# Gate-branch products woven into block 2's attention, and x and the first weights loaded in K pairs over two DMA queues

## The chip, the core and the metric

The kernel runs on one core of a Trainium2 chip. TensorE (PE) multiplies; VectorE (DVE), ScalarE (ACT) and GpSimd (POOL) work on tiles; SyncE (SP) issues nearly all DMAs. The metric is the device time of one execution in microseconds, as the median of several runs. PSUM holds the products, SBUF everything else.

## The reference

Two models run in a row on 256 rows of width 1024. The first has two layers: an RMS norm, a mixer of three attention branches with sigmoid gates, and a convolutional feed-forward. Its output goes through a final norm into the second, which has two layers over latents (256 rows) and a context (256 rows). The part that the change touches most is the second model's layer:

```
z = modulate(rmsnorm(x), shift, scale) @ w_in      # q, k, v, u, g for latents; context too, except in the last layer
attn = softmax(rope(rms(q)) rope(rms(k))^T) v      # 8 heads of 64; latents see 512 keys, the context 256
gm   = gelu(u) * (w_s @ layernorm(gelu(g)) + b_s)  # the gated branch ("gmlp"), 4 groups of 128 columns
x    = x + gate * (concat(attn, gm) @ w_out)
x    = x + gate2 * (square(relu(modulate(rmsnorm(x)) @ w_ff1)) @ w_ff2)
```

[...]

## The kernel before

`program` builds the instructions, and a scheduler orders them on each engine by priority (program order, unless `tc.high_priority` shifts it) and by when its own model of time holds them ready. That order is then fixed: each engine works through its queue in order. A tile pool gives `bufs` slots for each tag, and an instruction waits for a free slot.

**Weights.** `load_w` (line 134) starts one DMA of 1 MB from SP into `raw` (three slots), casts each half on ACT into `hi` (L147, 128x1024) and subtracts on DVE into `lo` (L149). With `by_piece`, used for the very first weights alone, each half has its own DMA, and the last two pairs of x tiles are loaded between them (L115). `mm3` (L157 to L159) issues the three passes of one K tile.

**Start.** `norm` (L451) splits each of the eight x tiles, scaled by the norm's gain, into the parts `e` (L184 on ACT, L185 on DVE), squares and adds them (L441, L443), and makes the row of inverse norms (L193 to L205). Then it loads the second weights and builds the normalised parts `h` (L466, L181, L182). Weight chunks below `EARLY` = 2 multiply `e` and scale the product by the row afterwards (L510); the others need `h`. In layer 0 the first chunk goes tile by tile, so all eight K tiles of its first half come before its second half; in layer 1 `zpair` takes both halves together, six K tiles and then two.

**Block 2, one layer.** After q, k and v come the g products (`g_half`, two halves of two groups each, GELU on ACT at L970). Then, in program order: the layer norm of g (L1049 to L1055), the u products (`u_tasks`: four tiles of eight K tiles, three passes, for each stream, 192 products in layer 0, which has two streams, and 96 in layer 1, which has one; GELU on ACT at L1066), and the attention. `attn` has a `front` (scores into `s`, row maximum on DVE at L1099, exponential on ACT at L363, scaling on ACT at L374) and a `back` (`pair_out`, L379): for each group of two key tiles, four transposes into `pt` (L388), a cast on ACT and a subtraction on DVE into two `kf` tiles (L181, L182), and six products with v into `o`. `pt` has one slot in PSUM, `s` two, `acc` four, and `kf` (the tag of `tmp()`) ten slots in SBUF. `pipelined` emits front i, then back i-1. A latent step has two groups, a context step one: 24 groups in layer 0 (8 latent and 8 context steps), 16 in layer 1 (8 latent steps).

`weave(attn(), fill, ratio)` takes `ratio` items of filler after each step. The filler is `mix_tasks` (four items, small products at L1077 and three DVE steps up to L1083 that build the gated branch) and then `out_half(1)` (eight tiles of 12 products, whose results update x at L1130). `out_half(1)` needs all four mix items.

```
def weave(main, side, ratio):
    due = 0.0
    for _ in main:
        due += ratio
        while due >= 1.0:
            next(side, None)
            due -= 1.0
    run(side)
```

Of the kernel before, what the change touches and what calls it, by code (L numbers as in the profile page):

```python
# [11 lines left out]
F32 = mybir.dt.float32  # L12
# [7 lines left out]
P = 128  # L20
# [9 lines left out]
EARLY = 2  # L30
# [9 lines left out]
WV2 = (0.78, 1.62)  # L40
# [5 lines left out]
XF = 4  # L46

WL = (1.0, 0.75)

PIPE = 1  # L50

# [20 lines left out]
def program(tc, A, out, stop=None):  # L72
# [10 lines left out]
    with top:  # L83
# [27 lines left out]
        par1 = const("par1")  # L111

        def load_x(k0, k1):
            for k in range(k0, k1, 2):
                nc.sync.dma_start(xx[:, k : k + 2, 0:T], A["xT"][:, k : k + 2, :])  # L115

        load_x(0, XF)
        ident = mk(cp, [P, P], tag="ident")
        make_identity(nc, ident)
        ones = mk(cp, [P, P], tag="ones")  # L120
        V.memset(ones, 1.0)
# [8 lines left out]


        last_lo, pin = [None], [None]

        def load_w(ap, *cuts, by_piece=False):

            raw = mk(wp, [P, 2048], tag="raw", bufs=3)
            if not by_piece:
                nc.sync.dma_start(raw[:, : cuts[-1]], ap)
            pieces, a = [], 0
            for b in cuts:  # L140
                if by_piece:
                    nc.sync.dma_start(raw[:, a:b], ap[:, a:b])
                    if a == 0:
                        load_x(XF, KD)
# [234 lines left out]
        def pair_out(po, ps, v, n):  # L379
# [3 lines left out]
            for g in range(0, n, 2):  # L383
# [50 lines left out]
        def block1():  # L434
            with ExitStack() as st:
# [15 lines left out]
                def norm(g, ap):  # L451
# [18 lines left out]
                for l in range(L):  # L470
# [13 lines left out]
                    def zpair(w, x):  # L484
                        ps = [acc()[:, :T] for _ in range(2)]
                        mm_pair(ps, w, x)
                        return ps

                    mod_rate(R1[l][0])
                    w0 = load_w(A["w_in"][l, 0], 1024, 2048, by_piece=l == 0)  # L490
# [4 lines left out]
                    hb = small([P, 24], tag="hb", bufs=2)  # L495
                    V.tensor_scalar_mul(hb, bgate, 0.5)
                    e, h, row, w1 = norm(n1g, A["w_in"][l, 1])


# [4 lines left out]
                    for c in range(3):  # L504
                        w = (w0, w1)[c] if c < 2 else wi(c)
                        first = zpair(w, e) if c == 0 and l else None
                        for mi in range(2):
                            j = 2 * c + mi
                            if c < EARLY:
                                V.tensor_mul(cz[:, j, :], first[mi] if first else ztile(w[mi], e), row)  # L510
# [862 lines left out]
```

## Time and profile before

| | us |
|---|---|
| median of 3 runs | 1806.24 |
| lowest and highest | 1802.46, 1807.23 |
| the profiled execution, its own time | 1804.39 |
| its span, first to last instruction | 1802.6 |
| PE busy in the span | 1750.1 (97%) |
| DVE busy | 1449.8 (80%) |
| ACT busy | 1014.0 (56%) |

The span is 1.8 us shorter than the execution's own time, and that execution is 1.85 us below the median. A PE that is shown busy is not PE at its peak: the end of a product is modelled, and a product after an idle stretch is shown longer than its step in a dense stream. So work on PE is counted below as products times the step from one start to the next in a dense stream.

### The profile page before, as it was taken

The page shows a single profiled execution, that of the slowest core. Times are in us where ns is not written, and L with a number is a line of the kernel's source. Part 1 is how long each engine was busy: PE and PEld are TensorE (multiplying, and loading weights), DVE is VectorE, ACT ScalarE, POOL GpSimd, SP SyncE. Part 2 cuts the span into 40 slices and gives each one's busy share as a digit, 9 for nine tenths or more (in the row PEclk, how much of TensorE's full clock was granted, in tenths as well). Part 3 has the DMA queues.
Part 4 walks back from the last instruction along what each step waited for, and adds up shares of the span by engine and source line. Part 5 has one row for each costly group of instructions (what it writes and reads, how often), then busy time and mean ns, then how long its engine had stood idle before and what let it go on. Part 6 is the DMA issues. An engine that isn't in the chain of part 4 may idle for free.

```text
span 1802.6 us, 33988 instructions
## 1 busy us (share of the span) xinstructions
PE 1750.1 (97%) x13352; PEld 1669.1 (93%) x13352; DVE 1449.8 (80%) x3142; ACT 1014.0 (56%) x1994; POOL 83.0 (5%) x85
## 2 busy tenths in 40 slices
PE   7999999999999999999999899999999999799999
PEld 6999999999999999999999677989898989689999
DVE  7996989889898788988778676988676768777665
ACT  5866656665585665766554575515151536665553
POOL 0100210000010021000012000000000001000000
PEclk9999999999999999999999999999999999999999
DMA  7364664557545456554533221554545443225552
GB/s 283 123 212 165 211 233 171 186 164 257 197 159 199 163 183 246 185 190 158 195 138 119 71 71 36 168 201 154 185 149 191 141 151 117 71 72 209 187 187 94
DMA packets 68096, 297.10 MB, mean 165 GB/s; under 512 B 7648, under 2 KB 11104, under 8 KB 42336
## 3 DMA queue, kind: packets, MB, share of 16 engines
q1 hardware_dynamic: 67936, 294.93, 47.4%
q8 instruction: 105, 1.72, 0.4%
q14 instruction: 55, 0.45, 0.1%
HBM read 293.85 MB, written 1.05 MB: 164 GB/s over the span
## 4 chain that ended last, share of the span: by engine, by line
PE 82%; DVE 9%; ACT 5%; issue 2%; POOL 1%; DMA 1%; SPq 0%; POOLq 0%; ACTq 0%; DVEq 0%
PE acc L157 24%; PE acc L158 23%; PE acc L159 23%; DVE lo L149 2%; PE s L157 2%; PE s L158 2%; PE s L159 2%; PE pt L388 1%; ACT hi L147 1%; DVE u L182 1%; PE o L158 1%; ACT p L363 1%; DVE mjunk L257 1%; ACT p L374 1%; PE o L157 1%
## 5 line engine op out<-in xcount | busy, mean ns | idle before, releaser
L157 PE MATMUL acc<-u,hi 128*128 128x256 f32 (+2 forms) x3604 | 1052.3, 293 | 17.5 <-ACT hi L147 10.3
L159 PE MATMUL acc<-u,lo 128*128 128x256 f32 (+2 forms) x3604 | 1048.7, 292 | 2.6 <-DVE lo L149 2.4
L158 PE MATMUL acc<-u,hi 128*128 128x256 f32 (+2 forms) x3604 | 1051.0, 292 | 0.0
L147 ACT CAST hi<-raw 128x1024 fp32r<-128x1024 f32 (+2 forms) x470 | 473.6, 1010 | 452.9 <-PE acc L158 383.8
L157 PEld LDWEIGHTS acc<-u,hi 128*128 128x128 f32 x3604 | 682.6, 190 | 33.5 <-ACT hi L147 11.4
L159 PEld LDWEIGHTS acc<-u,lo 128*128 128x128 f32 x3604 | 682.4, 190 | 16.7 <-DVE lo L149 4.2
L158 PEld LDWEIGHTS acc<-u,hi 128*128 128x128 f32 x3604 | 683.6, 190 | 13.6 <-DVE u L182 0.6
L149 DVE TENSOR_TENSOR lo<-raw,hi 128x1024 fp32r<-128x1024 f32 (+2 forms) x470 | 552.0, 1182 | 104.5 <-ACT hi L147 100.7
L257 DVE CUSTOM_DVE_ANT_0 mjunk<-mraw,csil,c_par 128x512 bf16<-128x512 f32 x160 | 120.7, 754 | 10.5 <-DMA mraw<-in_w_mod 9.8
L257 DVE CUSTOM_DVE_ANT_0 mjunk<-mraw,csil,mpart 128x512 bf16<-128x512 f32 x160 | 120.8, 755 | 7.9 <-DMA mraw<-in_w_mod 6.5
L1130 DVE SCALAR_TENSOR_TENSOR xx<-acc,mods,xx 128x256 f32<-128x256 f32 x144 | 64.7, 479 | 55.4 <-PE acc L159 55.2
L868 ACT ACTIVATE nt<-nt,shb 128x256 f32<-128x256 f32 x96 | 48.7, 510 | 61.0 <-DVE nt L867 60.9
L181 ACT CAST u<-nt 128x256 fp32r<-128x256 f32 x146 | 57.3, 405 | 41.0 <-DVE nt L1212 33.3
L195 POOL TENSOR_TENSOR rs_y<-rs_v,mhalf 128x2 f32<-128x2 f32 (+2 forms) x26 | 30.9, 1188 | 1019.3 <-DVE rs_v L193 1019.3
L182 DVE TENSOR_TENSOR u<-nt,u 128x256 fp32r<-128x256 f32 x146 | 59.4, 421 | 17.0 <-ACT u L181 15.6
L159 PE MATMUL s<-u,lo 128*128 128x256 f32 x224 | 62.9, 281 | 0.5 <-DVE lo L149 0.5
L157 PE MATMUL s<-u,hi 128*128 128x256 f32 x224 | 62.7, 280 | 0.0
L158 PE MATMUL s<-u,hi 128*128 128x256 f32 x224 | 62.7, 280 | 0.0
L1212 DVE TENSOR_TENSOR nt<-nt 128x256 f32<-128x256 f32 x96 | 40.5, 423 | 19.1 <-ACT nt L868 13.1
L157 PE MATMUL acc<-hi,u 128*128 128x256 f32 (+1 forms) x168 | 48.6, 289 | 0.0
L182 DVE TENSOR_TENSOR kf<-pt,kf 128x512 fp32r<-128x512 f32 x40 | 27.5, 688 | 26.2 <-ACT kf L181 26.0
L159 PE MATMUL acc<-hi,u 128*128 128x256 f32 (+1 forms) x168 | 48.2, 287 | 0.0
(243 smaller groups left out, 2048.7 us busy)
## 6 DMA issues: line engine op xcount, KB each, us to landing
raw<-in_w_ff SPq DMA_DIRECT2D x64, 1024.0 KB, 4.9
raw<-in_w_in SPq DMA_DIRECT2D x61, 1024.0 KB, 4.9
mraw<-in_w_mod SPq DMA_DIRECT2D x192, 256.0 KB, 3.4
raw<-in_w_up SPq DMA_DIRECT2D x44, 1024.0 KB, 4.9
raw<-in_w_down SPq DMA_DIRECT2D x32, 704.0 KB, 4.2
raw<-in_w_out SPq DMA_DIRECT2D x16, 1024.0 KB, 4.9
raw<-in_w_br SPq DMA_DIRECT2D x12, 1024.0 KB, 4.9
nbias<-in_na_bias SPq DMA_DIRECT2D x8, 384.0 KB, 3.0
```

Source lines behind the costliest of these rows:

```text
L147: S.copy(hi[:, : b - a], raw[:, a:b])
L149: last_lo[0] = V.tensor_sub(lo[:, : b - a], raw[:, a:b], hi[:, : b - a].bitcast(F32))
L157: PE.matmul(ps, a[0], b[0], start=start, stop=False)
L158: PE.matmul(ps, a[0], b[1], start=False, stop=False)
L159: return PE.matmul(ps, a[1], b[0], start=False, stop=stop)
L181: S.copy(hi, src)
L182: return V.tensor_sub(lo, src, hi.bitcast(F32))
L195: G.tensor_tensor(y, v, mhalf[:, :n] if len(shape)==2 else mhalf[:, :n].rearrange('p (a b) -> p a b', b=shape[2]), op=ALU.pow)
L257: V.tensor_tensor_reduce(out=junk, in0=w, in1=csil[:, i, half * 512 : half * 512 + 512], op0=ALU.mult, op1=ALU.add, scale=1.0, scalar=part ...
L868: S.activation(dst, dst, func, bias=b)
L1130: V.scalar_tensor_tensor(xx[:, m, cut(s)], ps[:, s * T - cols.start : s * T - cols.start + T], md[i][:, m, s : s + 1], xx[:, m, cut(s)], o ...
L1212: V.tensor_mul(r, r, r)
```

## The change

1. **Start.** `load_first` replaces `by_piece`: for K tiles 0-1, 2-3, 4-5 and 6-7 it loads both halves' columns of the first weights (the first piece from ACT's queue, the others from SP) and the two x tiles. `par1` comes in three DMAs, the eight columns that the first norm needs ahead. `split_first` casts and subtracts those pieces inside `norm`'s loop, and the first products take both halves two K tiles at a time. Four constants (`rope`, `gmask`, `fing`, `par2`) are loaded behind the norm. Eight products of a constant tile run on PE before any data is there.
2. **EARLY** is 3 in block 1's layer 0: chunk 2 multiplies `e` too, and its scaling by the row goes to DVE.
3. **Layer norm of g**: statistics directly behind each g tile, normalisation in two halves, the second behind the first u tile.
4. **u products as filler.** `mix_tasks` now makes the u tiles (`gate_tile`) and each mix one u tile later. Filler items: 16 in layer 0 (one is taken before the attention, then 1.0 a step), 12 in layer 1 (two before, then 1.55 a step). GELU becomes `twice_gelu`: a square and a tanh on ACT, three steps on DVE, with the factor one half in the mix.
5. **`pair_out`**: the six products with v get a priority 40 places later.
6. The attention's output takes the place of `q` (`ya = q`).

```diff
-EARLY = 2
+EARLY = (3, 2)
-WV2 = (0.78, 1.62)
+WV2 = (1.0, 1.55)
+NWARM = 8
+PRE = (1, 2)
+PVO = 40
...
+        idle = mk(pst, [P, 512], tag="pt")
+        for _ in range(NWARM):
+            PE.matmul(idle[:, 0:P], ones, ones, start=True, stop=True)
...
+        def load_first(ap):
+            raw = mk(wp, [P, 2048], tag="raw", bufs=3)
+            pieces = [(mk(wp, [P, 1024], F32R, tag="hi"), mk(wp, [P, 1024], F32R, tag="lo")) for _ in range(2)]
+            view = lambda t: t.rearrange("p (m c) -> p m c", m=2)
+            for k in range(0, KD, 2):
+                cs = slice(k * P, (k + 2) * P)
+                (nc.scalar if k == 0 else nc.sync).dma_start(view(raw)[:, :, cs], view(ap)[:, :, cs])
+                if k == 0:
+                    nc.sync.dma_start(par1[:, 0, 0:8], A["par1"][:, 0, 0:8])
+                load_x(k)
+            nc.sync.dma_start(par1[:, 0, 8:], A["par1"][:, 0, 8:])
+            nc.sync.dma_start(par1[:, 1, :], A["par1"][:, 1, :])
+            return raw, pieces
+        def split_first(raw, pieces, k):
+            for m, (hi, lo) in enumerate(pieces):
+                cs = slice(k * P, (k + 2) * P)
+                src = raw[:, m * 1024 + k * P : m * 1024 + (k + 2) * P]
+                S.copy(hi[:, cs], src)
+                last_lo[0] = V.tensor_sub(lo[:, cs], src, hi[:, cs].bitcast(F32))
...
-        def mm_pair(pss2, pieces, x, order=range(KD), late=2):
-            for part in (order[: KD - late], order[KD - late :]):
+        def mm_pair(pss2, pieces, x, order=range(KD), cuts=(0, 6, 8)):
+            for part in [order[a:b] for a, b in zip(cuts, cuts[1:])]:
...
-                for k in range(2):
-                    c = slice(k * T, k * T + T)
-                    mm3(po, v(g + k), (hi[:, c], lo[:, c]), g + k == 0, g + k == n - 1)
+                with tc.high_priority(offset=-PVO):
+                    for k in range(2):
+                        c = slice(k * T, k * T + T)
+                        mm3(po, v(g + k), (hi[:, c], lo[:, c]), g + k == 0, g + k == n - 1)
...
                     for k in range(KD):
+                        if first and k % 2 == 0:
+                            split_first(*first, k)
                         split(xx[:, k, 0:T], *e(k), g[:, k : k + 1])
...
-                        first = zpair(w, e) if c == 0 and l else None
+                        first = zpair(w, e, (0, 6, 8) if l else (0, 2, 4, 6, 8)) if c == 0 else None
...
+                            elif c < EARLY[l]:
+                                kz = mk(kp, [P, T], tag="nt", bufs=NT)
+                                V.tensor_mul(kz, ztile(w[mi], e), row)
+                                rope(kz, [kpe[:, 0, :], kpe[:, 1, :]], C, Sg, kp, NT)
...
+                    for _ in range(2):
+                        next(second)
+                        next(prep, None)
+                    normalise(0)
+                    weave(second, prep, 1.0)
...
+                    def twice_gelu(dst, x, n):
+                        th = tmp()[:, :n]
+                        S.activation(th, x, AF.Square)
+                        V.tensor_scalar(th, th, 0.044715 * GC, GC, op0=ALU.mult, op1=ALU.add)
+                        V.tensor_mul(th, th, x)
+                        S.activation(th, th, AF.Tanh)
+                        V.scalar_tensor_tensor(dst, th, 1.0, x, op0=ALU.add, op1=ALU.mult)
...
+                        def gate_tile(g):
+                            nonlocal w
+                            if g == 2:
+                                w = load_w(A["w_in2"][l, 4], 1024, 2048)
+                            us[g], ps = tmp(), acc()
+                            for s in streams:
+                                mm_x(ps[:, cut(s)], w[g % 2], (hl, hc)[s], T)
+                                if s != streams[-1]:
+                                    yield
+                            twice_gelu(us[g][:, full], ps[:, full], N)
+                            yield
...
+                        for g in range(4):
+                            yield from gate_tile(g)
+                            if g == 0:
+                                normalise(1)
+                            if g:
+                                mix(g - 1)
+                        mix(3)
...
-                    fill = chain(mix_tasks(), out_half(1, lambda k, c: gm[0](k, c), gate))
-                    run(u_tasks())
+                    fill = chain(mix_tasks(), out_half(1, gm, gate))
                     mod_rate(R2[1])
-                    ya = u8p()
+                    ya = q
+                    for _ in range(PRE[l]):
+                        next(fill)
                     weave(attn(), fill, WV2[l])
```

## Rows read from the trace of the kernel before

**Rows 1.** The page, part 1: busy time, share of the span, instructions of each engine

```profile
PE 1750.1 (97%) x13352; PEld 1669.1 (93%) x13352; DVE 1449.8 (80%) x3142; ACT 1014.0 (56%) x1994; POOL 83.0 (5%) x85
```

**Rows 2.** Windows: length; busy PE, PEld, DVE, ACT, POOL (count); clock, DMA, GB/s

```profile
30.00:60.00 30.00, 29.58 (x243) 28.69 (x242) 28.43 (x67) 17.16 (x36) 5.58 (x6) 1.00 0.59 214
978.00:1000.00 22.00, 22.00 (x187) 22.00 (x186) 18.50 (x59) 5.16 (x7) 3.33 (x1) 1.00 0.44 148
1000.00:1048.00 48.00, 38.76 (x208) 29.45 (x207) 28.84 (x62) 32.01 (x72) 0.00 (x0) 0.97 0.09 32
1048.00:1094.00 46.00, 46.00 (x255) 37.51 (x253) 35.17 (x82) 33.88 (x77) 1.90 (x2) 1.00 0.19 64
1526.40:1541.00 14.60, 13.17 (x106) 12.50 (x105) 11.28 (x44) 6.37 (x11) 3.56 (x3) 1.00 0.36 112
1541.00:1566.00 25.00, 16.71 (x84) 12.17 (x83) 18.00 (x38) 14.71 (x29) 0.29 (x1) 0.93 0.28 104
1566.00:1598.00 32.00, 31.76 (x237) 29.31 (x236) 25.02 (x53) 25.41 (x53) 0.00 (x0) 1.00 0.19 67
1598.00:1607.30 9.30, 6.19 (x38) 4.90 (x37) 2.55 (x5) 2.15 (x5) 0.00 (x0) 0.85 0.00 0
```

**Rows 3.** Two of these windows, scores `s` alone (PE, PEld, DVE, ACT)

```profile
1000.00:1048.00 48.00, 12.36 (x42) 7.49 (x42) 8.95 (x13) 11.35 (x32) 0.97 0.09 32
1541.00:1566.00 25.00, 6.30 (x21) 3.43 (x20) 4.71 (x7) 5.77 (x14) 0.93 0.28 104
```

**Rows 4.** The same two windows, transposes `pt` alone

```profile
1000.00:1048.00 48.00, 7.49 (x44) 5.45 (x44) 7.55 (x11) 6.39 (x11) 0.97 0.09 32
1541.00:1566.00 25.00, 3.42 (x19) 2.58 (x20) 2.75 (x4) 2.31 (x4) 0.93 0.28 104
```

**Rows 5.** The same two windows, products with v, `o`, alone

```profile
1000.00:1048.00 48.00, 12.07 (x60) 8.79 (x60) 2.08 (x5) 2.14 (x6) 0.97 0.09 32
1541.00:1566.00 25.00, 5.53 (x24) 3.98 (x24) 0.00 (x0) 0.10 (x1) 0.93 0.28 104
```

**Rows 6.** The same two windows, `acc` alone (filler and mixes)

```profile
1000.00:1048.00 48.00, 13.34 (x62) 9.14 (x61) 2.98 (x4) 0.59 (x1) 0.97 0.09 32
1541.00:1566.00 25.00, 2.88 (x20) 2.43 (x19) 1.34 (x3) 0.39 (x1) 0.93 0.28 104
```

**Rows 7.** Timeline of PE, layer 0's attention: start, length, instruction, idle before and releaser

```profile
1005.20 0.39 PE L158 MATMUL s<-kk,u 128*128 128x512 f32 x1
1005.43 0.39 PE L159 MATMUL s<-kk,u 128*128 128x512 f32 x1
...
1011.45 0.60 PE L388 MATMUL pt<-ident,kf 128*128 128x128 f32 x4
1012.72 0.38 PE L157 MATMUL o<-kf,vv 128*128 128x256 f32 x1 [0.68 <-ACT kf L181]
...
1014.14 0.60 PE L388 MATMUL pt<-ident,kf 128*128 128x128 f32 x4
```

**Rows 8.** Groups by line and shape, layer 0: busy, mean ns, idle before

```profile
L1066 ACT ACTIVATE u<-acc 128x512 f32<-128x512 f32 x4 | 2.4, 592 | 0.0
...
L1083 DVE TENSOR_TENSOR kf<-kf,u 128x512 f32<-128x512 f32 x4 | 2.7, 685 | 0.1
```

**Rows 9.** Timeline of the start, ACT and PE

```profile
4.36 0.51 ACT L184 ACTIVATE u<-xx,c_par 128x256 fp32r<-128x256 f32 x1 [2.12 <-DMA xx<-in_xT]
...
8.33 1.04 ACT L147 CAST hi<-raw 128x1024 fp32r<-128x1024 f32 x1 [0.89 <-DMA raw<-in_w_in]
...
9.43 0.58 PE L157 MATMUL acc<-u,hi 128*128 128x256 f32 x1 [9.43 <-ACT hi L147]
...
13.42 0.41 PE L159 MATMUL acc<-u,lo 128*128 128x256 f32 x1
...
18.50 0.37 ACT L205 COPY row<-o 128x256 f32<-128x256 f32 x1 [4.43 <-PE o L204]
18.77 2.00 ACT L147 CAST hi<-raw 128x1024 fp32r<-128x1024 f32 x2
```

More of the change, by code (lines that the diff above doesn't have):

```diff
@@ L109, in const, with load_x @@
             return t
[L111 to L117, printed above, removed]
+        par1 = mk(cp, list(A["par1"].shape), tag="c_par1", bufs=1)
+        def load_x(k):
+            nc.sync.dma_start(xx[:, k : k + 2, 0:T], A["xT"][:, k : k + 2, :])
+        ones = mk(cp, [P, P], tag="ones")
+        V.memset(ones, 1.0)
         ident = mk(cp, [P, P], tag="ident")
         make_identity(nc, ident)
-        ones = mk(cp, [P, P], tag="ones")
-        V.memset(ones, 1.0)
         mhalf = mk(cp, [P, 16], tag="mhalf")
@@ L449, in half4, with norm @@
                     return Parts([u8([P, 2, 4, T], F32R)])
-                def norm(g, ap):
+                def norm(g, ap, first=None):
                     e, h = pair8(), pair8()
@@ L482, in ztile, with zpair @@
                         return ps
-                    def zpair(w, x):
+                    def zpair(w, x, cuts=(0, 6, 8)):
                         ps = [acc()[:, :T] for _ in range(2)]
-                        mm_pair(ps, w, x)
+                        mm_pair(ps, w, x, cuts=cuts)
                         return ps
                     mod_rate(R1[l][0])
-                    w0 = load_w(A["w_in"][l, 0], 1024, 2048, by_piece=l == 0)
+                    if l == 0:
+                        first = load_first(A["w_in"][l, 0])
+                        w0 = first[1]
+                    else:
+                        w0, first = load_w(A["w_in"][l, 0], 1024, 2048), None
+                    hb = small([P, 24], tag="hb", bufs=2)
+                    V.tensor_scalar_mul(hb, bgate, 0.5)
+                    e, h, row, w1 = norm(n1g, A["w_in"][l, 1], first)
                     if l == 0:
@@ L970, in g_half, with normalise @@
                             S.activation(vg[0][:, b, c * T : (c + 1) * T], ps, AF.Gelu_apprx_tanh)
+                            for g in range(2):
+                                bn = small([P, 6], tag="bn", bufs=2)
+                                V.bn_stats(bn, vg[0][:, b, c * T + g * P : c * T + (g + 1) * P])
+                                V.bn_aggr(mv[:, b, g, :], bn)
                             yield
+                        rv = rsqrt(mv[:, 0:NB, :, 1], [P, NB, 2], 1.0, EPS)
+                        norms.append((mv, rv))
+                    norms = []
+                    def normalise(c):
+                        mv, rv = norms[c]
+                        for b in range(NB):
+                            for g in range(2):
+                                t = vg[0][:, b, c * T + g * P : c * T + (g + 1) * P]
+                                V.tensor_scalar(t, t, mv[:, b, g, 0:1], rv[:, b, g : g + 1], op0=ALU.subtract, op1=ALU.mult)
                     if l == 0:
@@ L1039, in block2 @@
                     wu = load_w(A["w_in2"][l, 3], 1024, 2048)
-                    weave(g_half(1, wg2), prep, 1.0)
-                    vg = vg[0]
+                    second = g_half(1, wg2)
+                    for _ in range(2):
[3 more added lines that the diff above has]
+                    weave(second, prep, 1.0)
                     if l == 0:
@@ L1070, in block2 @@
-                    gm = []
-                    def mix_tasks():
-                        gm[:] = [u8p()]
-                        for g in range(4):
+                    gm = u8p()
+                    def twice_gelu(dst, x, n):
[5 more added lines that the diff above has]
+                        V.scalar_tensor_tensor(dst, th, 1.0, x, op0=ALU.add, op1=ALU.mult)
@@ new lines, in mix_tasks, with mix @@
+                    def mix_tasks():
+                        us, w = {}, wu
+                        def gate_tile(g):
[9 more added lines that the diff above has]
+                            yield
+                        def mix(g):
```

50 lines of the change are left out of this document (10 added, 40 removed).

## The prediction

> **What bounds the kernel now.** I read the page's busy table first: PE is busy 97% of the span, DVE 80% [rows 1]. So a gain can only come from stretches in which PE stands, and a change that lays work on DVE has to be weighed there. The windows by stage come next, to find those stretches. While the u products run, 187 products take 22.00 us, 0.118 us each, and PE never stands [rows 2]. In layer 0's attention PE is busy 38.76 of 48 us from 1000 to 1048, then 46.00 of 46; in layer 1's 16.71 of 25 us from 1541 to 1566, then 31.76 of 32, then 6.19 of 9.3 [rows 2]. The same loop runs in all of them. What differs is the filler: few big products in the poor windows, many in the good ones [rows 2, 6].
>
> A standing PE is shown too busy, so I count work as products times step. Steps: 0.118 us for 256 columns, 0.23 for 512 (two scores in a row start 0.23 apart [rows 7]), about 0.09 for a transpose (the four at 1011.45 are shown as 0.60, most of it the tail of the last; 0.09 is my estimate, and 0.15 would be its upper end), 0.11 for a 128-column mix, taken as no longer than the 256-column step. Layer 0, 1000 to 1048: 42 scores 9.7, 44 transposes 4.0, 60 products with v 7.1, 32 mixes 3.5, 30 filler products at up to 0.23, 6.9; together 31.2 of 48 us, **16.8 lost** [rows 3 to 6]. Layer 1, 1541 to 1566: 21 scores 4.8, 19 transposes 1.7, 24 products 2.8, 16 mixes and 4 products 2.2; 11.5 of 25, **13.5 lost** [rows 3 to 6]. Around it layer 1 loses 1.4 (1526.4 to 1541), 0.2 and 3.1 more, **18.2** in 80.9 us [rows 2].
>
> Why: with no filler the attention is a ring. One group goes from its transposes at 1011.45 to the next group's at 1014.14, 2.69 us, of which PE works 4 x 0.09 + 6 x 0.118 = 1.07. The products wait 0.68 us for the cast on ACT, and `pt` has one slot, so the next transposes wait too [rows 7]. **1.6 us of each group is exposed.**
>
> At the start PE makes its first product at 9.43 us, behind the cast of the first half megabyte, which ACT begins at 8.33 when the data is there; x was there at 4.36 [rows 9]. At 13.42 a product of 256 columns is still shown at 0.41 us, where one of 512 columns takes 0.39 later [rows 7, 9]: PE is at 1.2 GHz there, the lower of its two levels.
>
> **The change, part by part.**
>
> *Layer 0, u products as filler.* 192 products, 22.6 us, move from ahead of the attention into it; their total stays. They depend on nothing in the attention, so they can lie in the 1.6 us of every group, which the lower priority of the v products asks for. Added on ACT: a square and a tanh where one GELU took 0.592 us, four tiles, +2.4 us; on DVE three steps of 0.685, four tiles, +8.2 us [rows 8]. Counted over 978 to 1094 (116 us), PE's work is 116 - 16.8 = 99.2; DVE's 18.50 + 28.84 + 35.17 + 8.2 = 90.7; ACT's 5.16 + 32.01 + 33.88 + 2.4 = 73.5 [rows 2]. If the stage takes 103 us, DVE is at 88%. That lies between two stages that keep PE full: this loop at 1048 to 1094 with DVE at 76%, and block 1 at 30 to 60 us with DVE at 95% and PE at 29.58 of 30 [rows 2]. So I leave 3.8 us of the 16.8 lost: **-13 us**. Ends: all of it, -16.8; and DVE bound at 76%, 90.7/0.76 = 119 us, +3.
>
> *Layer 1.* 96 products, 11.3 us, move likewise, two of four tiles ahead of the attention. PE's work is 80.9 - 18.2 = 62.7; DVE's 11.28 + 18.00 + 25.02 + 2.55 = 56.9, plus 4 x 3 half-wide steps at half of 0.685, 4.1: 61 us [rows 2, 8]. Now DVE is level with PE. At block 1's 95% the stage would take 64, at the 78% of 1566 to 1598 78 us. I take 72, between them: **-9 us**, ends -17 and -3. ACT has 49.1 us there, 1.0 to 1.8 more with the second table function, and is not the bound [rows 2, 8]. The drain behind the last filler (6.19 busy of 9.3) stays: the last items are given out by step 7 of 8.
>
> *Statistics of g earlier, normalisation in halves:* the same steps on DVE; they leave the front of the attention for the g products. Nothing where DVE has room there, and I credit nothing. `ya = q`: no instruction. The second half of the normalisation now stands in DVE's queue behind the first u tile's three steps, and mixes 2 and 3 wait for it; u tiles 2 and 3 cover that (5.7 us in layer 0).
>
> *The start.* The first K pair is 512 KB with x, so ACT can begin about when it does now, 4.4 to 5 us. From there ACT paces: eight splits and eight squares at no more than 0.51, at most 8.2 us, and 2.0 us of casts (two at 1.00 each, as at 18.77 [rows 9]), up to twice that in quarter tiles: it ends at 15 to 17 us. The first 48 products end 1.4 us later, instead of shortly before 19.8 (the next weights' cast starts at 18.77 and takes 1.0 [rows 9]). Three things decide what is left: whether those casts pass the row copy, which stands 4.43 us at ACT's head [rows 9] (if not, they come up to 1 us later than now, since the row does); that chunk 2 no longer waits for `h`; and that DVE, which gets some 1.7 us more, works at 95% right behind [rows 2]. **-2.5 us**, ends +1 and -5 (first product at 4.4 instead of 9.43). The constants behind the norm pass the second weights in SP's queue; their first user, the rope of chunk 2, is over 15 us away. The DMA issue on ACT stands where ACT waits 2.12 us for x anyway. The eight constant products run before data is there and hold nobody; if they raise the clock, little is won, since ACT needs some 2.5 us for each K pair, and PE's 12 products take 2.8 at twice 0.118.
>
> A rule speaks against the second queue. The row shows the first cast waiting for its data until 8.33 [rows 9]. The Trainium skill, DMA: Bandwidth & Descriptors, section "Issuing engines are not separate DMA queues", has DMAs of all engines share the same 16 engines, so that only issue time is saved. By it the start would come from the order of the pieces alone; if that gave nothing, the sum would be 2.5 us smaller, 22.
>
> **Sum.** -13 - 9 - 2.5 = -24.5. The profiled execution took 1804.4 in all (span 1802.6 and 1.8 around it), so 1779.9; it lay 1.85 below the median of 1806.24, so about **1782** as a median.
>
> **Rivals.**
>
> *DVE takes PE's place.* For: 61 us of DVE against 62.7 of PE in layer 1, 90.7 against 99.2 in layer 0. Against: 95% with PE full at 30 to 60 [rows 2]. Layer 1 gains 3, layer 0 gains 5, the start 2.5: 1796.
>
> *Nearly all is won:* 16.8 + 17 + 5 = 38.8, plus clock, since the windows at 0.93 to 0.97 would stay at 1.00 [rows 2]: about 1766. Against: the drains stay, and each step's chain runs over three engines.
>
> *The start doesn't do what it says,* since w1's casts stay behind the row: 1784 to 1785, inside my range.
>
> *Slower: the queues of ACT and DVE and the ten `kf` slots choke the ring.* GELU's chain now crosses ACT and DVE four times, 2 x 0.592 + 3 x 0.685 = 3.2 us with no handover counted [rows 8], and each link stands ahead of some group's cast. Slots: four score tiles of two steps, four parts of two groups, two u tiles, one for the tanh, one for the mix are 12 of 10. If a group's cast waits behind that chain or for a slot, its 1.6 us is exposed again, filler or not. All 40 groups would cost 64 us; today's loss, 16.8 + 18.2 = 35, is worth 22 groups. Above 22 exposed groups the attention is slower than now; with all 40, +29 - 2.5: 1833. With 30, +13 - 2.5: 1817. Against it: 1048 to 1094 holds the same groups beside filler and loses nothing [rows 2]. The order in a queue does bind: at 18.50 ACT stood 4.43 us at the row while casts that it could have done stood behind [rows 9]. The Trainium skill says that too, in TensorE: Matmul & The Clock Gate, "Architectural detail", where ScalarE's and VectorE's queues are strictly first in, first out; by it each late link would cost what stands behind it, as priced here.
>
> **How the numbers follow.** About 0.3%, 5.4 us, is what a measurement of this kernel can tell from no change. Chances: forecast (1773 to 1790, the start's failure included) 0.55; DVE in PE's place (1790 to 1800) 0.17; nearly all won (below 1773) 0.10; within 5.4 us of now 0.07; slower by the choked ring 0.11. So faster 0.82, same 0.07, slower 0.11. The range 1763 to 1799 leaves out the last two and the edges of the others.
>
> **What would show it.** In the profile after, right: no stretch of the attention in which PE's work is under nine tenths of the time, scores and transposes with `acc` products between, as now at 1048 to 1094; the stretch that is now 978 to 1094 in layer 0 near 103 us instead of 116, layer 1's 1526.4 to 1607.3 near 72 instead of 80.9; the first product at 5 to 6 us, the second chunk's at 16 to 20. Wrong: DVE above 95% in the attention and PE waiting for DVE lines; `o` products still waiting for `kf` casts at L181 in most groups; score products waiting for `kf` slots; a late row in the start. The forecast falls if the scheduler's model puts the u products in one block ahead of the attention, as it could if it believes the ring free of gaps: then only the start is left, 1804.

## The result and the profile after

| | us |
|---|---|
| before, median of 4 runs | 1804.95 |
| after, median of 4 runs | 1786.82 (1785.11 to 1787.39) |
| ratio after to before | 0.9902, 95% interval 0.9888 to 0.9915 |
| the profiled execution after: its own time, its span | 1786.61, 1784.8 |

So 18 us are gone (0.98% of 1805 is 17.7, interval 15.3 to 20.2), where 24.5 were forecast. The predicted range holds the time; over a quarter of the forecast gain did not come, and the stages tell where.

The page after, part 1 (engine, busy us, share, instructions):

```profile
PE 1750.1 (98%) x13368; PEld 1673.0 (94%) x13368; DVE 1458.6 (82%) x3176; ACT 1017.7 (57%) x2007; POOL 83.5 (5%) x87
```

PE's busy time is that of [rows 1] to the tenth, DVE has 9 us more. The windows of the stages after, columns as in [rows 2]. The first two rows are the two attentions, each from about the last g product to about the last product with v; the next four are pieces of layer 0's, the last two lie in layer 1's.

```profile
972.20:1084.00 111.80, 104.58 (x653) 90.36 (x653) 91.51 (x212) 74.48 (x162) 3.53 (x3) 0.97 0.21 71
1511.70:1586.60 74.90, 67.11 (x460) 59.85 (x458) 59.12 (x141) 50.00 (x99) 3.94 (x4) 0.95 0.24 85
...
976.00:985.00 9.00, 4.99 (x37) 4.56 (x35) 8.38 (x25) 1.03 (x3) 1.64 (x1) 0.98 0.44 146
985.00:1025.00 40.00, 39.68 (x284) 36.65 (x284) 32.39 (x74) 29.59 (x65) 0.00 (x0) 0.96 0.24 80
1025.00:1040.00 15.00, 12.11 (x57) 9.40 (x58) 11.00 (x23) 10.22 (x24) 0.00 (x0) 0.89 0.06 19
1040.00:1084.00 44.00, 44.00 (x248) 35.99 (x247) 35.94 (x79) 30.55 (x68) 1.90 (x2) 1.00 0.21 72
...
1518.00:1532.00 14.00, 9.98 (x50) 8.55 (x49) 11.98 (x33) 7.14 (x13) 2.00 (x2) 0.76 0.21 76
1532.00:1555.00 23.00, 19.94 (x133) 16.79 (x131) 19.38 (x44) 16.56 (x37) 0.00 (x0) 1.00 0.26 92
```

The middle of layer 0's attention, where PE was busy 38.76 of 48 us [rows 2], is now shown full: 39.68 of 40 and 44.00 of 44. Counted as products times step, 3.4 us of those 40 are lost and 1.2 of those 44, where 16.3 of the 48 were (16.8 by the prediction's count). Most of what is left sits in few places: 976 to 985 (4.6 us lost), 1025 to 1040 (5.8), and in layer 1's attention 1518 to 1555 (13.0). What PE waits for there, summed by line (waiter, releaser: us in total, times, longest); first layer 0's attention before; then, after, layer 0's and below the dots layer 1's:

```profile
PE o L158 <- DVE kf L182: 4.2, 8, 1.0
PE o L157 <- ACT kf L181: 2.5, 4, 0.7
```

```profile
PE s L180 <- ACT kf L386: 4.3, 2, 4.0
PE acc L180 <- DVE kf L1108: 1.8, 1, 1.8
PE pt L411 <- ACT kf L397: 0.4, 1, 0.4
PE o L181 <- DVE kf L205: 0.3, 1, 0.3
...
PE acc L180 <- DVE kf L1108: 2.1, 1, 2.1
PE acc L1129 <- DVE kf L1108: 2.0, 2, 1.5
PE o L181 <- DVE kf L205: 1.7, 3, 1.0
```

Read them as the prediction asked: the products with v no longer wait for their casts in layer 0 (6.7 us became 0.3), so the filler does cover the ring. Two new waits took a part of that. One, 1.8 us, is for L1108, the last of the five steps of `twice_gelu`. The other, 4.0 us for the first exponential (L386), is one place, seen best in DVE's timeline (start, length, instruction, idle before and releaser):

```profile
976.87 0.40 PE L182 MATMUL s<-kk,u 128*128 128x512 f32 x1
976.96 2.34 DVE L172 TENSOR_TENSOR lo<-raw,hi 128x1024 fp32r<-128x1024 f32 x2
...
980.42 1.20 DVE L172 TENSOR_TENSOR lo<-raw,hi 128x1024 fp32r<-128x1024 f32 x1
981.60 1.29 DVE L1158 TENSOR_REDUCE nm<-s 128x1 f32<-128x512 f32 x2
983.97 0.78 ACT L386 ACTIVATE kf<-s,nm,sc 128x512 f32<-128x512 f32 x1 [8.28 <-DVE nm L1166]
984.89 0.80 PE L180 MATMUL s<-kk,u 128*128 128x512 f32 x1 [4.01 <-ACT kf L386]
```

The second score tile of the first step is done at 977.3; its row maximum starts behind three subtractions of weights, a modulation and statistics, and PE, whose order has the third score tile next, stands with u products still to do. In the kernel before, the 192 u products stood ahead of the first scores, and DVE did such work under them; the change took that cover away.

**How the stages are compared.** The changed kernel and `free_acc` below have the same order of PE's products up to block 2, and yet their first g products stand at 946.32 and 944.35 us. Of that, 1.7 us open between 738 and 838: PE waits for nothing there and its granted clock is 1.00 in both, but its products start every 0.118 us in the one and every 0.116 in the other. PE's clock, too, falls to its lower level in other places from one execution to the next. So each layer is measured from its own last g product to the first column sum behind its `out_half(0)`. In brackets stands the time lost: the sum over PE's products of the distance to the next start, less the step (0.118 us for 256 columns, 0.233 for 512, 0.11 for 128; four transposes in a dense stretch take 0.36, not 0.44, so 1 to 2 us too little is shown in each attention, in every kernel alike).

| kernel | ratio to before | layer 0: to first score, to last v product, to column sum | sum | layer 1, the same | sum |
|---|---|---|---|---|---|
| before | 1 | 23.1 (0.3), 97.0 (18.6), 22.0 (7.8) | 142.2 | 7.2 (0.5), 72.1 (20.1), 15.7 (3.5) | 94.9 |
| `start_only` | 0.9982 | 23.1 (0.3), 96.8 (18.3), 21.2 (6.9) | 141.0 | 7.2, 72.0 (20.0), 15.6 | 94.8 |
| after | 0.9902 | 3.0 (0.0), 108.8 (15.0), 20.0 (1.4) | 131.8 | 6.3 (0.0), 68.6 (16.1), 15.4 (3.2) | 90.3 |
| `block2_only` | 0.9925 | as after | 131.5 | as after | 90.2 |
| `pvo0` | 0.9957 | 3.0, 111.9 (16.4), 20.1 (3.0) | 134.9 | 6.3, 73.4 (20.9), 15.3 | 95.0 |
| `reduce_first` | 0.9894 | first score 7.0 ahead of the last g product | 128.6 | likewise, 2.1 ahead | 89.5 |
| `free_acc` | 0.9874 | 3.0, 102.5 (8.7), 20.1 (1.4) | 125.6 | 6.3, 69.1 (16.6), 15.4 | 90.8 |
| `no_gelu_steps` | 0.9845 | 3.0, 103.3 (9.5), 20.1 | 126.4 | 6.3, 64.9 (12.4), 15.4 | 86.6 |
| `real_gelu` | 0.9886 | 3.0, 105.7 (11.9), 20.1 | 128.8 | 6.3, 67.6 (15.1), 14.1 | 87.9 |
| `free_acc_pre3` | 0.9870 | 3.0, 103.8 (9.9), 20.1 | 126.9 | 6.3, 69.0 (16.5), 15.4 | 90.7 |
| `free_acc_pre3_max` | 0.9877 | first score 7.0 ahead of the last g product | 126.1 | 6.3, 69.3 (16.8), 14.0 | 89.6 |
| `free_acc_norm_act` | 0.9879 | 3.0, 105.0 (11.1), 20.0 | 128.0 | 6.4, 67.8 (15.3), 15.4 | 89.6 |

Three kernels with the same block 2 as after (`block2_only`, `row_dve`, `no_warm`) give 131.5 to 131.8 and 90.2 to 90.3, where a ratio has an interval of some 2.5 us to each side. But a stage can move by more where PE's clock falls in other places of it: `free_acc` and `free_acc_pre3` have the same layer 0 and give 125.6 and 126.9 (at the lower level from 984.2 to 987.6 in the one, from 982.9 to 989.8 in the other), `free_acc_pre3` and `free_acc_pre3_max` all but the same layer 1 and give 90.7 and 89.6, and before and `start_only` the same block 2 and give 142.2 and 141.0 in layer 0. After the same wait of 1.3 us behind layer 1's last product with v, the granted clock up to the column sum is 0.89 in one and 1.00 in the other. So differences of up to 1.3 us between stages are not told apart below.

### The profile page after: what moved, and what is told of

The parts are those of the page before. It is cut to its first block, busy times and chain, and to the rows that moved or that the text cites. A ratio compares the mean times of both kernels' runs of the same rounds, so it can differ in the third digit from the quotient of the medians.

```text
span 1784.8 us, 34096 instructions
## 1 busy us (share of the span) xinstructions
PE 1750.1 (98%) x13368; PEld 1673.0 (94%) x13368; DVE 1458.6 (82%) x3176; ACT 1017.7 (57%) x2007; POOL 83.5 (5%) x87
## 4 chain that ended last, share of the span: by engine, by line
PE 80%; DVE 11%; ACT 5%; issue 2%; POOL 1%; DMA 0%; POOLq 0%; ACTq 0%; DVEq 0%
PE acc L180 23%; PE acc L182 23%; PE acc L181 23%; DVE lo L172 3%; PE s L180 2%; PE s L181 2%; PE s L182 2%; DVE u L205 1%; PE pt L411 1%; POOL rs_y L218 1%; ACT hi L170 1%; ACT p L386 1%; ACT p L397 1%; PE o L180 1%; DVE mjunk L280 1%
## 5 line engine op out<-in xcount | busy, mean ns | idle before, releaser
L181 PEld LDWEIGHTS acc<-u,hi 128*128 128x128 f32 x3604 | 682.8, 189 | 16.2 <-DVE u L208 1.9
L182 PEld LDWEIGHTS acc<-u,lo 128*128 128x128 f32 x3604 | 682.1, 189 | 15.1 <-DVE lo L172 2.1
L172 DVE TENSOR_TENSOR lo<-raw,hi 128x1024 fp32r<-128x1024 f32 (+2 forms) x468 | 551.2, 1184 | 101.7 <-ACT hi L170 95.8
L218 POOL TENSOR_TENSOR rs_y<-rs_v,mhalf 128x2 f32<-128x2 f32 (+2 forms) x29 | 35.2, 1215 | 1080.3 <-DVE rs_v L216 1080.3
L205 DVE TENSOR_TENSOR u<-nt,u 128x256 fp32r<-128x256 f32 x146 | 59.5, 421 | 17.2 <-ACT u L204 15.7
L181 PE MATMUL acc<-lo,u 128*128 128x256 f32 (+1 forms) x168 | 48.1, 286 | 0.0
```

The costliest lines, as they stand in the source:

```text
L172: last_lo[0] = V.tensor_sub(lo[:, : b - a], raw[:, a:b], hi[:, : b - a].bitcast(F32))
L181: PE.matmul(ps, a[0], b[1], start=False, stop=False)
L182: return PE.matmul(ps, a[1], b[0], start=False, stop=stop)
L205: return V.tensor_sub(lo, src, hi.bitcast(F32))
L218: G.tensor_tensor(y, v, mhalf[:, :n] if len(shape)==2 else mhalf[:, :n].rearrange('p (a b) -> p a b', b=shape[2]), op=ALU.pow)
```

## The experiments

**The two halves of the change.** `start_only` is the kernel before with the start alone (points 1 and 2 of the change), `block2_only` has all the rest. The rest reaches block 1 as well, since block 1's attention calls `pair_out` too, whose products with v come later: the order of PE's products there differs in 334 places. With `PVO = 0`, which puts them back, the first g product stands at 946.30 against the changed kernel's 946.32.

> The kernel before with the start alone: first weights and x in K pairs over two queues, the eight constant products, chunk 2 before the normalisation; block 2 as before. Theory A (the start is worth what stands between the two traces when the g products begin, 945.73 against 951.53 and 972.16 against 976.88, and all of that comes from the start): 4.7 to 5.8 us less than before. Rival B (only the 2.9 us that are there at 30 us come from the start, what is added later in block 1 comes from elsewhere or is noise of the profile): 2.5 to 3.2 us less. Rival C (my forecast's worst end): 0 to 1 more.

> The kernel before with the changes of block 2 alone (u products as filler, statistics of g earlier, normalisation in halves, lower priority of the products with v, output in q's place); the start as before. Theory A: the rest of the 18.1 us, 12.3 to 13.4 less than before, so that the two halves add up. Rival B: 15 less. If the halves do not add up to 18.1 within 1.5 us, one of them changes what the other gives.

Measured: 0.9982 (0.9973 to 0.9992), 3.2 us less (1.4 to 4.9); and 0.9925 (0.9910 to 0.9940), 13.5 less (10.8 to 16.2). Together 16.8, against 17.7 for the whole: the halves add up. B's 2.5 to 3.2 us lie in the first interval; theory A's 4.7 is at its very edge. The trace cannot decide: in the profiled execution of `start_only` the same product stands 2.6 us earlier than before at 26 us, 0.6 to 0.8 from 66 to 471 (its clock is at the lower level from 27.4 to 30.8), and 2.0 at the last g product of layer 0.

**The start, one step further.** In the changed kernel the first product of data starts at 5.61 instead of 9.43 us, and the 48th at 14.43 instead of 19.22; but at the 96th only 1.4 us of that are left, at the 144th 2.3. ACT and PE there:

```profile
13.68 1.05 ACT L170 CAST hi<-raw 128x1024 fp32r<-128x1024 f32 x1 [1.02 <-DMA raw<-in_w_in]
16.82 0.37 ACT L228 COPY row<-o 128x256 f32<-128x256 f32 x1 [2.10 <-PE o L227]
17.09 1.05 ACT L170 CAST hi<-raw 128x1024 fp32r<-128x1024 f32 x1
...
18.20 0.38 PE L180 MATMUL acc<-u,hi 128*128 128x256 f32 x1 [1.17 <-ACT hi L170]
```

The second cast of the second weights waits behind the row copy, as one of the three open points of the prediction had it. `row_dve` takes the copy off ACT (`V.tensor_copy` for `S.copy` in `rows_of`, for the first row alone).

> The changed kernel with one more edit: the copy of the first row of inverse norms goes from ACT to DVE. In the changed kernel ACT stands 2.10 us at that copy, from 14.7 to 16.8, while the second half of the second weights lies in SBUF and waits behind it, and PE then stands 1.17 us for that half and falls to the low clock level from 18.7 to 22.1 us. Theory A (that place in ACT's queue is what takes back the start's gain): 1.2 to 2.7 us less than the changed kernel. Rival B (DVE, busy right behind, paces the start anyway): within 0.5 us of the changed kernel.

Measured: 0.9907 (0.9893 to 0.9921), not to be told from the changed kernel's 0.9902; the intervals allow some of A's range too, but the trace shows B. The two casts now follow each other, and the next thing is late, in the same place:

```profile
13.65 1.99 ACT L170 CAST hi<-raw 128x1024 fp32r<-128x1024 f32 x2 [0.53 <-DMA raw<-in_w_in]
...
17.25 2.35 DVE L172 TENSOR_TENSOR lo<-raw,hi 128x1024 fp32r<-128x1024 f32 x2
...
18.52 0.58 PE L182 MATMUL acc<-u,lo 128*128 128x256 f32 x1 [1.18 <-DVE lo L172]
```

The subtractions stand on DVE behind the row, which waited 0.90 us for POOL; 1.17 us of waiting became 1.18.

`no_warm` leaves out the eight products of a constant tile (`NWARM = 0`).

> The changed kernel without the eight products of a constant tile. Theory A (my forecast: they hold nobody and win little, because ACT's 2.0 us for each K pair paces the first 48 products): 0 to 0.6 us more than the changed kernel, with PE at the low clock level at 5 us and at the full one by about 10. Rival B (they raise the clock for all of the first chunk, and 12 products at 0.212 us, 2.5 us, would be slower than ACT's pair): 1.5 to 2.5 us more.

Measured: 0.9914 (0.9901 to 0.9928); by the ratios 2.2 us more than the changed kernel, inside the intervals, so the times allow A and B. The trace speaks for A: the products of the first chunk start every 0.21 us until 10.9 (the lower clock level, 1.2 GHz), where the changed kernel's start every 0.12 us from 6.4 on; yet the 48th product comes at 14.41 us against 14.43, and the 144th at 31.87 against 32.07. ACT and DVE pace the chunk. The eight products do not raise the clock reliably either: in the traces of `row_dve` and `free_acc_pre3`, which have them, the full level comes at 10.6 and 10.2 us, in the changed kernel and `free_acc` by 5.1 and 4.6. The 48th product starts between 14.28 and 14.52 in all four.

**The lower priority of the products with v.** `pvo0` has `PVO = 0`.

> The changed kernel with the lower priority of the products with v taken back (offset 0 instead of 40). Theory A (the u products come between the transposes and the products with v only because these are asked to come later): products with v wait again for the cast and the subtraction of their tiles in part of the 40 groups, as in the kernel before (6.7 us in layer 0), 5 to 15 us more than the changed kernel. Rival B (the scheduler's model of time fills the gaps by itself): within 2 us.

Measured: 0.9957 (0.9942 to 0.9972), by the ratios 9.9 us more than the changed kernel; the stages give 3.1 and 4.7. By the time that is A: this one number carries over half of what block 2's part won. In layer 1 nothing is left (95.0 against 94.9 before), and its products with v wait again, 4.4 us where the changed kernel has 2.1. In layer 0 they do not, 0.7 us against 0.3, so there B holds: the order fills the ring without the lower priority, and of the 3.1 us 1.4 are lost up to the last product with v and 1.6 behind it. PE, layer 1:

```profile
1541.66 0.28 PE L182 MATMUL o<-kf,vv 128*128 128x256 f32 x1
1542.38 0.38 PE L180 MATMUL o<-kf,vv 128*128 128x256 f32 x1 [0.44 <-ACT kf L204]
1543.72 0.39 PE L181 MATMUL o<-kf,vv 128*128 128x256 f32 x1 [0.96 <-DVE kf L205]
```

**The first row maxima.** `reduce_first` puts the maxima of each layer's first step 100 places earlier:

```diff
+                            soon = tc.high_priority(offset=100) if (j, side, b) == (0, 0, 0) else nullcontext()
...
+                                with soon:
+                                    for i in range(2):
+                                        V.tensor_reduce(nm[:, i : i + 1], src[i], ...)
```

> The changed kernel with one edit: in block 2's attention the two row maxima of each layer's first step get a priority 100 places higher. In the changed kernel layer 0's first scores are done at 977.3, but their row maxima stand in DVE's queue behind three casts of weights, a modulation and the statistics of g until 981.60, and PE, which has no filler ready in its own order, stands 4.01 us for the exponential and runs at the low clock level from 984.9 to 987.2. Theory A (that place in DVE's queue is the largest new wait of layer 0): 3 to 5.5 us less than the changed kernel. Rival B (a maximum that stands earlier in DVE's queue only makes DVE stand there until the scores come, since DVE is busy throughout): within 1 us.

Measured: 0.9894 (0.9879 to 0.9909), 1.4 us less by the ratios, inside the intervals; the stages give 3.2 and 0.8 less, the second no more than the clock's places make. Between A and B: the first scores moved up with the maxima, to 7.0 us ahead of the last g product, so this is not a clean test of the place in the queue.

**The slot in `acc`, or DVE's load.** `twice_gelu` reads its product from PSUM in the first, third and fifth of its steps, so the `acc` slot is taken until the fifth. `free_acc` copies it out first; `no_gelu_steps` leaves the GELU out (a square in its place, so it computes something else); `real_gelu` uses ACT's own function.

```diff
 def twice_gelu(dst, x, n):
     th = tmp()[:, :n]
+    S.copy(dst, x)                                   # free_acc
+    x = dst                                          # free_acc
     S.activation(th, x, AF.Square)
...
+    S.activation(dst, x, AF.Square)                  # no_gelu_steps, the one step
+    S.activation(dst, x, AF.Gelu_apprx_tanh)         # real_gelu, the one step
```

> The changed kernel with one edit: the u tile is first copied on ACT from PSUM to its SBUF tile, and the five steps of the GELU read that copy, so that its acc slot comes free after one ACT step instead of after five steps over two engines. ACT does four copies more a layer (0.6 us each in layer 0, 0.4 in layer 1). Theory A (the slot is what PE waits for: 1.81 us in layer 0, 1.49, 2.12 and 0.49 in layer 1, each released by the last of the five steps): 3 to 6 us less than the changed kernel, 3 to 4 of it in layer 1. Rival B (DVE's load paces the stage, the slot is only where it shows): within 1 us, or up to 2 more, since nothing leaves DVE.

> The changed kernel with the GELU of the u tiles left out: one square on ACT takes its place, so that the three DVE steps and the tanh of each of the eight tiles are gone (on DVE some 8 us in layer 0, 4 in layer 1). The output is another one. Theory A (the acc slot): about what the earlier release gives, 3 to 6 us less than the changed kernel. Rival B (DVE's load): clearly more than that, 8 to 12 us less, near my forecast of the two layers. Theory C (neither; the places in DVE's queue of maxima and casts): less than 2.

> The changed kernel with the u tiles' GELU made by one ACT instruction, as in the kernel before, so that nothing is added on DVE; the exponential and the GELU then take turns on ACT, which loads its table anew each time (1.28 us for a load in the trace). Eight tiles with up to two loads each are up to 20 us on ACT, less two steps of 0.4 to 0.6 each. Theory A (the acc slot): the slot is free after one step, but exponentials and casts stand behind the loads; between 2 less and 5 more than the changed kernel. Rival B (DVE's load): 3 to 8 less.

Measured: `free_acc` 0.9874 (0.9857 to 0.9891), some 5 us less than the changed kernel (the two intervals just touch); `no_gelu_steps` 0.9845 (0.9826 to 0.9864), some 10 less; `real_gelu` 0.9886 (0.9871 to 0.9900), some 3 less, inside the intervals. The stages say more than the sums. In layer 0 `free_acc` wins 6.2 us with nothing taken off DVE (4.9 by `free_acc_pre3`, the same layer 0 again), and leaving all the steps out wins no more (5.4): there it was the slot. PE's waits in layer 0's attention in `free_acc`, and the two windows:

```profile
PE s L180 <- ACT kf L386: 4.0, 1, 4.0
```

```profile
970.00:1075.50 105.50, 101.46 (x653) 90.29 (x652) 91.25 (x213) 76.48 (x166) 3.54 (x3) 0.98 0.22 76
1503.20:1578.60 75.40, 67.29 (x461) 61.03 (x459) 59.45 (x141) 51.75 (x103) 4.20 (x4) 0.93 0.23 85
```

Every wait but the one at the head is gone, the ones between pieces of the ring too, and with them the low clock at 1035.9 to 1039.3. I had put 1.81 us of the gain there and 3 to 4 in layer 1; in layer 1 it gave nothing (0.5 more). There A fails: the waits for L1108 went, and one of 4.9 us for L172 came in their place. In layer 1 the kernels with less on DVE are faster: `no_gelu_steps` by 3.7, `real_gelu` by 2.4, of which 1.3 lie behind the last product with v, where the clock did not fall. That fits B, but does not show it. With the steps, two things go: DVE's work, and the wait of each mix, and so of `out_half(1)`, for the chain. In the changed kernel the last u product starts 24.8 us behind the last g product and the first of `out_half(1)` 35.8; between them PE has little to fill with. In `no_gelu_steps` the second comes at 32.3, and 2.6 of the 3.7 us are won between the first product with v and that place. No run parts the two. For `no_gelu_steps` I gave B 8 to 12 us in all. That number came (10 by the ratios, 9.1 by the stages), but by luck: 5.4 of it lie in layer 0, where freeing the slot alone wins as much.

**What holds layer 1.** `free_acc_pre3` asks for the second u weights ahead of the attention (`PRE = (1, 3)`, `WV2 = (1.0, 1.4)`); `free_acc_pre3_max` adds the earlier maxima in layer 0; `free_acc_norm_act` moves the normalisation of g from DVE to ACT:

```diff
-V.tensor_scalar(t, t, mv[:, b, g, 0:1], rv[:, b, g : g + 1], op0=ALU.subtract, op1=ALU.mult)
+S.activation(t, t, AF.Identity, bias=nb[:, b, g : g + 1], scale=rv[:, b, g : g + 1])
```

> The kernel with the early copy out of PSUM (free_acc), and in layer 1 three filler items ahead of the attention instead of two, then 1.4 a step instead of 1.55; layer 0 as in free_acc. There, PE's one wait of 4.9 us in layer 1 is for the first weight remainder of the second two u tiles: its subtraction stands on DVE behind the first step's row maxima and their scaling, since those weights are asked for only after the first step. With a third item ahead, they are asked for before it. Theory A (the order in DVE's queue): the 4.9 us go, 2 to 4 us less than free_acc, since the first maxima then stand behind two subtractions of 1.2 us. Rival B (DVE's load): the wait moves to another place of the stage, within 1 us of free_acc.

> The kernel free_acc_pre3 with, in layer 0 alone, the first step's row maxima 100 places earlier. In free_acc PE's only wait over 0.25 us in layer 0's attention is 4.15 us for the first exponential, behind those maxima. Theory A (the order in DVE's queue): 2 to 4 us less than free_acc_pre3. Rival B (the maxima ahead of the statistics and casts make these late, so that the wait moves): within 1 us.

> The kernel free_acc with the normalisation of g on ACT: of each layer's two halves, the steps on DVE (16 of 128 columns in layer 0, 8 in layer 1, about 0.27 us each in a row, 4 and 2 us) become as many on ACT, and one small step on DVE for each half makes their bias. In the changed kernel DVE is busy 15.05 of 16 us at the head of layer 0's attention (972 to 988) and 17.56 of 20 in layer 1 (1512 to 1532), and ACT 6.74 and 10.38. Theory A (DVE's load at the two heads holds what is left of the waits): layer 1's wait of 4.9 us for the weight remainder shrinks by up to 2 us and layer 0's of 4.15 by up to 1; 1 to 3 us less than free_acc. Rival B (only the order in DVE's queue, that is the maxima and subtractions themselves): the waits stay within 0.5 us, the time within 1.

Measured: 0.9870 (0.9854 to 0.9886), 0.9877 (0.9861 to 0.9893) and 0.9879 (0.9863 to 0.9896), none to be told from `free_acc`. Layer 1 in `free_acc`, then in `free_acc_pre3`:

```profile
PE acc L182 <- DVE lo L172: 4.9, 1, 4.9
PE o L180 <- ACT kf L204: 1.6, 2, 1.3
```

```profile
PE s L180 <- ACT kf L386: 2.7, 2, 1.9
PE acc L1131 <- DVE kf L1133: 2.2, 1, 2.2
PE acc L180 <- ACT u L204: 1.3, 1, 1.3
PE acc L182 <- DVE lo L172: 1.1, 1, 1.1
```

Another order splits the wait and the stage stays (90.8, 90.7), as B had it. In layer 0 the earlier maxima change as little once the slot is free (126.9, 126.1): the wait of 4.0 us became waits of 2.4, 1.9 and two smaller ones. Taking the 2 us of normalisation off DVE shortened layer 1 by 1.2 us, but its wait for the weight remainder only from 4.9 to 4.6 (B's half microsecond, not A's two), and the clock falls once less in that execution, so the 1.2 are not shown to be the edit's. In layer 0 the same edit cost 2.4 (1.1 against `free_acc_pre3`), and the wait for the first exponential grew from 4.0 to 6.1, since the small step that makes the bias stands on DVE ahead of the maxima and waits for POOL:

```profile
983.50 0.17 DVE L1013 SCALAR_TENSOR_TENSOR nb<-mv,rs_y 128x8 f32<-128x8 f32 x1 [1.52 <-POOL rs_y L218]
983.59 1.28 DVE L1162 TENSOR_REDUCE nm<-s 128x1 f32<-128x512 f32 x2
```

The best kernels of the study are `free_acc` and `free_acc_pre3`, at 0.987 of the time before, some 5 us below the changed one. A kernel with ACT's own GELU in layer 1 alone and the early copy in layer 0 might take the better half of each; it was not run.

## Why the prediction was right, and where its sum was not

**The mechanism.** A ring with 1.6 us exposed in each group, covered by products from elsewhere: shown in layer 0, where the waits of the products with v fell from 6.7 to 0.3 us and the middle loses 3.4 of 40 us instead of 16.3 of 48. That it takes the lower priority, as the prediction had it, is shown for layer 1 alone (`pvo0`). How much the cover is worth was another matter, as the next two paragraphs say. One sign of being right failed: from 1025 to 1040 PE's work is 9.3 of 15 us, far under nine tenths. The slower rival, the ring choked by the queues, did not come about; what is real in it is two places, 4.0 and 1.8 us, not 22 groups. No score product waits for a `kf` slot.

**Layer 0, -13 forecast, -10.4 measured** (142.2 to 131.8; 9.2 against `start_only`, whose block 2 is that of before). The work on the engines was right: DVE 90.7 forecast, 91.51 measured; ACT 73.5 and 74.48. (Layer 1's 49.1 us for ACT are 48.6 by [rows 2]; nothing hangs on it.) Up to the last product with v, which is what the forecast was for, the stage shrank by only 8.4 us, and 4.4 of these are work that left it: in PE's order 132 products of 512 columns stood ahead of the last v product before, 113 after, and the 19 that moved behind it fill the drain. The windows of the drain, before and after, columns as in [rows 2]:

```profile
1097.00:1119.00 22.00, 18.21 (x111) 16.42 (x110) 18.31 (x47) 14.40 (x35) 0.00 (x0) 0.84 0.18 61
...
1084.60:1104.60 20.00, 19.40 (x130) 17.33 (x129) 17.78 (x45) 13.54 (x32) 0.00 (x0) 1.00 0.20 66
```

So by the time lost the attention gave 3.9 us (18.9 to 15.0) and the drain 6.4 (7.8 to 1.4). The sum had nothing for the drain and said that the drains stay; that layer 0's total comes near -13 is luck in its greater part. The 3.8 us that I left as lost were far too few: the stretches with the two waits, 976 to 985 and 1025 to 1040, alone lose 10.4. Neither is DVE's share, by which I chose the number; `free_acc` keeps DVE's work (91.25 us) and the stage falls to 125.6, 16.6 below before, of which the attention's lost time gives 10.2 and the drain's 6.4. So what the term left out was not the load but two things that hung on the order: who holds the `acc` slot, and what stands ahead of the first maxima once the u products no longer cover them. The prediction counted the chain of GELU as 3.2 us that cross ACT and DVE four times, and used it for the slower rival alone; it did not ask which PSUM slot is taken for that long.

**Layer 1, -9 forecast, -4.6 measured.** Here a step was wrong: "96 products, 11.3 us, move likewise, two of four tiles ahead". PE's order before has 52 products of 256 columns between the last g product and the first score and 176 from there to the last v product; after, 48 and 180. So 44 of the 96 u products, all but four of those that the change meant to move, already stood behind the first score, though in one dense block from 1535.57 to 1540.91 us and not in the gaps of the ring; what the change did was to spread them. At most 48 products, 5.7 us, could so come to lie in gaps: less than the 9 that were forecast, and far from the end of -17. The trace before would have told, with the first score at 1533.48 and that block behind it, in a window that loses only 1.4 us [rows 2]. The rival with DVE in PE's place gave layer 1 a gain of 3, nearer than the forecast; the 3.7 us that come when the GELU steps go fit it, without showing that it is DVE's load and not the length of the chain. Why a wait of about 5 us at this head only changes its place under another order is not settled; DVE is busy 11.98 of 14 us there, and the 16 groups' exposed time, 25.6 us, is more than the filler (48 u and 96 other products of 0.118 us and 16 mixes of 0.11, 18.8).

Layer 1's drain behind the last filler stayed, as said (3.5 us lost, then 3.2).

**The start, -2.5 forecast, -3.2 measured (1.4 to 4.9).** Its parts: first product 5.61 (5 to 6 said), the second chunk's from 16.5 (16 to 20 said). The 48th product was better than said (14.43; 16 to 18 was the forecast for the end of the first chunk), in part because the casts of the quarter pieces are 0.70 us a pair and not twice 1.0. Of the three open points, the casts did stay behind the row copy (2.10 us), and it did not matter, since DVE's subtractions come as late (`row_dve`). The Trainium skill, TensorE: Matmul & The Clock Gate, section "Architectural detail", calls ACT's and DVE's queues strictly first in, first out; both traces of the start agree, with a cast and then a subtraction that stand behind work that waits for another engine. What the second DMA queue by itself gives was not run.

## What to carry to other kernels

Before a filler is priced, count on PE's own order where its products stand now and how many the change can bring into gaps: here that count bounds layer 1's gain at 5.7 us where 9 were forecast. Count the stretch behind the last of the main work too, since filler that moves there wins as well: 6.4 of layer 0's 10.4 us. Then ask what the filler covered where it was, and which PSUM slot its results hold, and for how many steps; a copy out of PSUM ahead of a chain over two engines cost nothing that the stages tell and won 5 to 6 us in layer 0, about half as much again as the plain filler. A wait that only changes its name when the order is changed may be a load or the length of a chain: in layer 1 only leaving the steps out won clearly more.

## What the runs showed of the hardware

- A table load on ACT takes 1.283 us. `real_gelu` has 19 of them, 12 more than the changed kernel, some 15 us on ACT (the two lines with most of them are below), and was no slower than the five steps over two engines: 0.9886 against 0.9902 of the time before, and 3.0 and 2.4 us less in the two stages, a part of it because the clock falls less there. Where ACT waits for nothing else, it stands under 0.05 us on either side of a load, so a switch costs about the load itself. A dear instruction on an engine with room can be as cheap as three on one without.

```profile
L386 ACT ACT_TABLE_LOAD x9 | 11.5, 1283 | 2.3 <-DVE nm L1161 2.1
L1103 ACT ACT_TABLE_LOAD x6 | 7.7, 1283 | 0.1
```

- Waits of PE cost more than their length. After the 4.0 us at 980.9 the products of 512 columns start every 0.43 us until 987.2, where 0.23 is their step: some 1.2 us on top (the granted clock is at its lower level from 984.7 to 988.1). In the start the window 14 to 25 has a granted clock of 0.84, behind waits of 1.3 and 1.2 us.
- Two executions with the same order of PE's products can differ where PE hardly waits (0.2 us at most): between 738 and 838 us PE's dense products start every 0.116 us in ten of the profiled kernels and every 0.118 in four (`after`, `start_only`, `no_gelu_steps` and `free_acc_norm_act`), with a granted clock of 1.00 in all. That makes 1.7 us; no run shows why.
